# Hybrid decoder layer: the statistics of the query and key norm are copied out of PSUM with epsilon added, and the logarithm and the correction read the copy

## The chip, the core and the metric

The kernel runs on one core of a Trainium2 chip. A core has TensorE (PE, matrix products, results go to PSUM), VectorE (DVE), ScalarE (ACT), GpSimd (POOL) and SyncE (SP, which here issues most DMA transfers). Each engine works through a queue of its own in order; engines wait for each other by semaphores. The metric is the device time of one execution in microseconds (us), the median of several runs.

## What is computed

One inference step of one layer of a decoder for 520 tokens (512 of a prompt, 8 single decode tokens): an input projection, attention with 16 heads of 64 beside a short convolution, an output projection and an MLP. What matters here is the norm of the queries and keys, per head over its 64 elements:

```python
EPS = 1e-6
def _rmsnorm(x, g):
    xf = x.astype(jnp.float32)
    y = xf * lax.rsqrt(jnp.mean(xf * xf, axis=-1, keepdims=True) + EPS)
    return (y * g.astype(jnp.float32)).astype(x.dtype)

    q = _rmsnorm(q.reshape(b, s, N_HEADS, HEAD_DIM), q_g)
    k = _rmsnorm(k.reshape(b, s, N_HEADS, HEAD_DIM), k_g)
```

## The kernel before

Activations lie transposed, features on the 128 partitions and the 520 tokens in two halves of 260 columns (`HT`). A product of fp32 accuracy is made of three products of split operands (high x high, high x low, low x high). Weights come by DMA in tiles of 128 x 1024 (`raw`) and are split on the chip: ACT rounds the high part (L148), VectorE subtracts it to get the low part (L149). `block` (L210) issues six products for 128 rows of a tile, three split terms for each of the two halves; TensorE's products of the projections are at L213.

The order of work on every engine is the order in which the program issues it; it was written by hand. Small work of the attention is threaded between the products of the projections by generators: `block` calls `step` (L183) after every third product, and a `step` advances first the norm at the head of the queue `bgn` and then the generator at the head of `bg` by one `yield` each. `wait(n)` (L197) yields n times, so what stands behind `wait(3)` is issued nine products later than what stands before it. Being issued later does not by itself make work start later: it only stands behind more work in its engine's queue.

For each of eight pairs of heads j the projection makes q, k and v in turn. `ev_qkv` (L523) takes a result out of PSUM with VectorE (L530; for the first v at L528), squares it for q and k on ACT (L535) and GpSimd (L537, L538), and puts a `norm_gen` (L404) into `bgn` to start 24 steps later (30 for the first pair). `norm_gen` handles the two halves one after the other. Per half: two products with `bd`, a block-diagonal matrix of 1/64, put the mean squares of each head into a PSUM tile `st` (L408; it is taken from `pw`, which has two buffers); three steps later ACT takes the logarithm of mean plus epsilon (L411) and the exponential of -0.5 times that (L412), which gives a first reciprocal root r0; then VectorE makes one step of Newton's method and applies the gain (L414 to L417). After another three steps the second half or the end follows: ACT and VectorE split the normalised tile into high and low part (L419, L420). L414 is the last reader of `st`. The tiles r0 and t1 are in SBUF (name `h`, four buffers).

`attn_gen(j)` (L425) is queued when v of the pair is done. It waits in the program until both norms of j have been issued, then transposes the decode tokens' columns of q, k and v (L433, the second transpose reads the finished k) and v (L440), makes scores (L456), softmax (L463 to L473), transposes the probabilities into `pw` or `pS` tiles (L480), takes these out as high part on ACT (L483) and low part on VectorE (L484), and multiplies with v (L490); L495 and L496 take that result out. While the attention of pair j runs, the norms of pair j + 1 follow once the scores of j have been issued.

Of the kernel before, what the change touches and what calls it, by code (L numbers as in the profile page):

```python
# [25 lines left out]
F32 = mybir.dt.float32  # L26
F32R = mybir.dt.float32r
AF = mybir.ActivationFunctionType
OP = mybir.AluOpType
# [6 lines left out]
HT = TOK // 2  # L36
# [6 lines left out]
EPS = 1e-6  # L43
# [41 lines left out]
def hymba_kernel(ctx, tc, xT, wi, wo, wu, wd, state_k, state_v, sconv, relb, relrep, ohp, lcp, ohd, lcd,  # L85
                 gains, qkg, convw, yT, okT, ovT, ocp, oks, ovs, ocs):
    nc = tc.nc
    V, S, P, T, SP = nc.vector, nc.scalar, nc.gpsimd, nc.tensor, nc.sync
# [3 lines left out]
    wk = ctx.enter_context(tc.tile_pool(name="wk", bufs=1))  # L92
# [15 lines left out]
    def flat(t):  # L108
        return t.rearrange("p a b -> p (a b)")
# [87 lines left out]
    def wait(n):  # L197
        for _ in range(n):
            yield
# [4 lines left out]
    def wtile():  # L204
        return p2.tile([128, 512], F32, name="pw", bufs=2)
# [60 lines left out]
    epst = cst.tile([128, 1], F32, name="epst")  # L266
# [137 lines left out]
    def norm_gen(j, raw, sq, gain, hi, lo, k_out):  # L404
        for t in range(2):
            st = wtile()
            for i in range(2):
                T.matmul(st[:, :HT], bd, sq[i][:, t, :], start=i == 0, stop=i == 1)  # L408
            yield from wait(3)
            r0 = wk.tile([128, HT], F32, name="h", bufs=4)  # L410
            S.activation(r0, st[:, :HT], AF.Ln, bias=epst)  # L411
            S.activation(r0, r0, AF.Exp, scale=-0.5)  # L412
            t1 = wk.tile([128, HT], F32, name="h", bufs=4)
            V.scalar_tensor_tensor(t1, st[:, :HT], EPS, r0, op0=OP.add, op1=OP.mult)  # L414
            V.scalar_tensor_tensor(raw[:, t, :], raw[:, t, :], gain, r0, op0=OP.mult, op1=OP.mult)
            V.scalar_tensor_tensor(t1, t1, -0.5, r0, op0=OP.mult, op1=OP.mult)
            V.scalar_tensor_tensor(raw[:, t, :], t1, 1.5, raw[:, t, :], op0=OP.add, op1=OP.mult)  # L417
            yield from wait(3)
        S.activation(hi, flat(raw), AF.Copy)  # L419
        V.tensor_tensor(lo, flat(raw), hi.bitcast(F32), OP.subtract)  # L420
        if k_out is not None:
            SP.dma_start(k_out, flat(raw)[:, :SEQ])
        done["norm", j] = done.get(("norm", j), 0) + 1
# [99 lines left out]
    def ev_qkv(t, j, ps):  # L523
        raw = wt(name="raw")
        RAW[t, j] = raw
        if isinstance(ps, tuple):
            for h in range(2):
                V.tensor_tensor(raw[:, h], ps[h][:, :HT], rstd[:, h], OP.mult)  # L528
        else:
            V.tensor_tensor(raw, ps[:, :, :HT], rstd, OP.mult)  # L530
        if t == 1 and j:
            load_T(j)
        if t < 2:
            sh, sl_ = (wk.tile([128, 2, HT], F32R, name="sq", tag=g_, bufs=n_) for g_, n_ in (("w", 16), ("g", 4)))
            S.activation(sh, raw, AF.Square)  # L535
            sq = wt(name="tmp")
            P.tensor_tensor(sq, raw, raw, OP.mult)  # L537
            P.tensor_tensor(sl_, sq, sh.bitcast(F32), OP.subtract)  # L538
            hi, lo = (qh, ql) if t == 0 else (kh, kl)
            bgn.append([24 if j else 30, j, norm_gen(j, raw, (sh, sl_), qkgt[:, t:t + 1], hi, lo, okT[:, j] if t else None)])  # L540
        else:
            SP.dma_start(ovT[:, j], flat(raw)[:, :SEQ])
            bg.append(attn_gen(j))
# [534 lines left out]
    for n in range(7 * NG):  # L1078
# [18 lines left out]
        if kind == "up":  # L1097
# [27 lines left out]
            if gi == 2 and pi == 4:  # L1125
                st = p3.tile([128, 2, 512], F32, name="mn", bufs=2)
# [130 lines left out]
```

## Time and profile before

| | us |
|---|---|
| median of 3 runs (2150.16 to 2151.25) | 2150.71 |
| the profiled execution | 2150.38 |
| its span, first to last instruction | 2148.4 |
| TensorE busy in the span | 2129.5 |
| VectorE busy | 1758.7 |
| ScalarE busy | 957.8 |
| GpSimd busy | 56.6 |

The granted clock of TensorE is 1.00 in the whole span. The times of the projection of q, k and v with the norms and the attention of the prompt are about 47 to 405 us of the span. Times in the rows are microseconds from the start of the span. In a timeline a row gives start and length, the engine, the line, the operation, what it writes and reads and how many instructions it stands for; square brackets at its end give how long the engine had stood idle before it and for whom. Starts are exact; the lengths of neighbouring instructions overlap where an engine begins one before the last has been written out.

### The profile page before, as it was taken

The page shows a single profiled execution, that of the slowest core. Times are in us where ns is not written, and L with a number is a line of the kernel's source. Part 1 is how long each engine was busy: PE and PEld are TensorE (multiplying, and loading weights), DVE is VectorE, ACT ScalarE, POOL GpSimd, SP SyncE. Part 2 cuts the span into 40 slices and gives each one's busy share as a digit, 9 for nine tenths or more (in the row PEclk, how much of TensorE's full clock was granted, in tenths as well). Part 3 has the DMA queues.
Part 4 walks back from the last instruction along what each step waited for, and adds up shares of the span by engine and source line. Part 5 has one row for each costly group of instructions (what it writes and reads, how often), then busy time and mean ns, then how long its engine had stood idle before and what let it go on. Part 6 is the DMA issues. An engine that isn't in the chain of part 4 may idle for free.

```text
span 2148.4 us, 42322 instructions
## 1 busy us (share of the span) xinstructions
PE 2129.5 (99%) x17594; PEld 2103.1 (98%) x17594; DVE 1758.7 (82%) x2423; ACT 957.8 (45%) x1379; POOL 56.6 (3%) x81
## 2 busy tenths in 40 slices
PE   8999999999999999999999999999999999999999
PEld 8999999999999999999999999999999999999999
DVE  7777777697787657798888888888999999999997
ACT  5544444312123245554444444445444444444443
POOL 1010100000000000000000000000000000000000
PEclk9999999999999999999999999999999999999999
DMA  5354444476554647588785676676876666666653
GB/s 209 128 177 164 167 137 148 137 228 200 164 187 170 225 166 259 187 275 273 282 273 197 236 266 210 237 271 219 319 280 235 241 229 237 239 233 234 244 200 108
DMA packets 138367, 461.40 MB, mean 215 GB/s; under 512 B 19552, under 2 KB 49888, under 8 KB 131776
## 3 DMA queue, kind: packets, MB, share of 16 engines
q1 hardware_dynamic: 136320, 454.81, 60.7%
q0 software_dynamic: 1296, 3.67, 0.9%
q8 instruction: 138, 2.26, 0.4%
q14 instruction: 53, 0.43, 0.1%
q10 hardware_dynamic: 560, 0.22, 0.0%
HBM read 415.88 MB, written 181.16 MB: 278 GB/s over the span
## 4 chain that ended last, share of the span: by engine, by line
PE 89%; DVE 6%; ACT 2%; DMA 2%; issue 1%; SPq 0%; DVEq 0%; ACTq 0%
PE mn L1023 30%; PE mm L1023 29%; PE mm L213 26%; DMA raw<-wi 2%; DVE wlo L149 1%; PE pS L456 1%; PE pS L490 1%; DVE R L788 1%; PE pw L480 1%; ACT whi L148 1%; DVE x1t L927 0%; DVE acc L920 0%; DVE wlo L788 0%; ACT sq L918 0%; DVE kv L664 0%
## 5 line engine op out<-in xcount | busy, mean ns | idle before, releaser
L213 PE MATMUL mm<-R,whi 128*128 128x260 f32 x4000 | 676.6, 286 | 5.7 <-ACT whi L148 5.4
L213 PEld LDWEIGHTS mm<-R,whi 128*128 128x128 f32 x4000 | 559.4, 189 | 19.1 <-issue 8.6
L1023 PE MATMUL mm<-R,whi 128*128 128x260 f32 x3008 | 547.7, 283 | 1.2 <-ACT cs L1106 1.2
L1023 PE MATMUL mn<-R,whi 128*128 128x260 f32 x3008 | 547.7, 283 | 0.2 <-DVE yacc L1143 0.2
L1023 PEld LDWEIGHTS mm<-R,whi 128*128 128x128 f32 x3008 | 463.3, 188 | 1.5 <-ACT cs L1106 1.4
L1023 PEld LDWEIGHTS mn<-R,whi 128*128 128x128 f32 x3008 | 463.3, 188 | 0.4 <-issue 0.4
L1023 PE MATMUL mn<-R,wlo 128*128 128x260 f32 x1504 | 424.8, 282 | 0.7 <-DVE wlo L788 0.7
L1023 PE MATMUL mm<-R,wlo 128*128 128x260 f32 x1504 | 425.0, 283 | 0.4 <-DVE wlo L788 0.4
L213 PE MATMUL mm<-R,wlo 128*128 128x260 f32 x2000 | 403.1, 283 | 0.0
L788 DVE TENSOR_TENSOR wlo<-raw,whi 128x1024 fp32r<-128x1024 f32 x255 | 311.8, 1223 | 110.0 <-ACT whi L787 107.9
L787 ACT ACTIVATE whi<-raw 128x1024 fp32r<-128x1024 f32 x255 | 269.3, 1056 | 206.0 <-PE mn L1023 94.5
L213 PEld LDWEIGHTS mm<-R,wlo 128*128 128x128 f32 x2000 | 309.2, 189 | 0.4
L787 ACT ACTIVATE whi<-rg 128x1024 fp32r<-128x1024 f32 x186 | 197.3, 1061 | 217.0 <-PE mn L1023 87.5
L1023 PEld LDWEIGHTS mn<-R,wlo 128*128 128x128 f32 x1504 | 283.1, 188 | 0.9 <-DVE wlo L788 0.9
L1023 PEld LDWEIGHTS mm<-R,wlo 128*128 128x128 f32 x1504 | 283.1, 188 | 0.7 <-DVE wlo L788 0.6
L788 DVE TENSOR_TENSOR wlo<-rg,whi 128x1024 fp32r<-128x1024 f32 x186 | 226.5, 1218 | 2.1 <-ACT whi L787 2.0
L148 ACT ACTIVATE whi<-raw 128x1024 fp32r<-128x1024 f32 (+1 forms) x129 | 133.7, 1038 | 165.4 <-PE mm L213 129.7
L149 DVE TENSOR_TENSOR wlo<-raw,whi 128x1024 fp32r<-128x1024 f32 (+1 forms) x129 | 155.4, 1205 | 41.6 <-ACT whi L148 39.3
L841 DVE TENSOR_TENSOR raw<-raw 128x1024 f32<-128x1024 f32 x64 | 78.0, 1218 | 0.0
L841 DVE TENSOR_TENSOR raw<-rg,raw 128x1024 f32<-128x1024 f32 x62 | 76.0, 1225 | 2.1
L841 DVE TENSOR_TENSOR rg<-rg,raw 128x1024 f32<-128x1024 f32 x62 | 75.5, 1218 | 0.0
L1143 DVE TENSOR_TENSOR yacc<-mm,yacc 128x520 f32<-128x520 f32 x96 | 66.6, 694 | 7.0 <-PE mm L1023 6.0
(231 smaller groups left out, 2267.4 us busy)
## 6 DMA issues: line engine op xcount, KB each, us to landing
oks<-state_k SPq DMA_DIRECT2D x184, 356.0 KB
ovs<-state_v SPq DMA_DIRECT2D x184, 356.0 KB
raw<-wi SPq DMA_DIRECT2D x94, 512.0 KB
raw<-wu SPq DMA_DIRECT2D x64, 512.0 KB
rg<-wd SPq DMA_DIRECT2D x64, 512.0 KB
raw<-wd SPq DMA_DIRECT2D x64, 512.0 KB
rg<-wu SPq DMA_DIRECT2D x60, 512.0 KB
raw<-wo SPq DMA_DIRECT2D x32, 512.0 KB
```

The lines of the kernel that those rows point to most:

```text
L148: S.activation(his[i][:, h], raws[i][:, h], AF.Copy)
L149: V.tensor_tensor(los[i][:, h], raws[i][:, h], his[i][:, h].bitcast(F32), OP.subtract)
L213: T.matmul(ps[t][:, :HT] if isinstance(ps, tuple) else ps[:, t, :HT], a[:, k, :], b[:, t, :], start=start and n == 0, stop=stop and n == 2)
L456: T.matmul(ss[hp][:, :w], a[r, q], b[r, :w], start=n == 0, stop=n == 2)
L480: T.transpose(st[:, s * 128:(s + 1) * 128], lg[:, s * 128:(s + 1) * 128], ident)
L490: T.matmul(st[:, s * 128:], vv[:, hp, s].rearrange("p c e -> p (c e)"), b[:, s, s * 128:], start=s == 0 and n == 0, stop=s == 3 and n == 1 ...
L787: S.activation(hi, src, AF.Copy)
L788: eng.tensor_tensor(lo, src, hi.bitcast(F32), OP.subtract)
L841: V.tensor_tensor(o_, a_, b_, op)
L1023: T.matmul(ps[:, r, :HT], a[:, k, :], b(kt), start=n % 7 in ((0, 1, 3) if kts == 8 else (0, 1)) and kt == 0 and m == 0, stop=kt == kts - 1 ...
L1143: V.tensor_tensor(dst[:, r], v[:, r], dst[:, r], OP.add)
```

## The change

The two statements of `norm_gen` that read `st` become one. An addition on VectorE, issued right behind the products and ahead of the three steps of waiting, writes mean plus epsilon to the SBUF tile t1. The logarithm reads t1 instead of `st` and has no bias operand any more. Where L414 had added epsilon and multiplied by r0 in one instruction on `st`, a multiplication of t1 by r0 remains. t1 is taken from `h` before r0 instead of after it. The other VectorE steps, and everything else, stay.

```diff
             st = wtile()
             for i in range(2):
                 T.matmul(st[:, :HT], bd, sq[i][:, t, :], start=i == 0, stop=i == 1)
+
+            t1 = wk.tile([128, HT], F32, name="h", bufs=4)
+            V.tensor_scalar(t1, st[:, :HT], EPS, None, op0=OP.add)
             yield from wait(3)
             r0 = wk.tile([128, HT], F32, name="h", bufs=4)
-            S.activation(r0, st[:, :HT], AF.Ln, bias=epst)
+            S.activation(r0, t1, AF.Ln)
             S.activation(r0, r0, AF.Exp, scale=-0.5)
-            t1 = wk.tile([128, HT], F32, name="h", bufs=4)
-            V.scalar_tensor_tensor(t1, st[:, :HT], EPS, r0, op0=OP.add, op1=OP.mult)
+            V.tensor_tensor(t1, t1, r0, OP.mult)
             V.scalar_tensor_tensor(raw[:, t, :], raw[:, t, :], gain, r0, op0=OP.mult, op1=OP.mult)
             V.scalar_tensor_tensor(t1, t1, -0.5, r0, op0=OP.mult, op1=OP.mult)
             V.scalar_tensor_tensor(raw[:, t, :], t1, 1.5, raw[:, t, :], op0=OP.add, op1=OP.mult)
```

## Rows read from the trace of the kernel before

**Rows 1.** The page: busy time of TensorE and its weight loads, share of the span.

```profile
PE 2129.5 (99%) x17594; PEld 2103.1 (98%) x17594; DVE 1758.7 (82%) x2423; ACT 957.8 (45%) x1379; POOL 56.6 (3%) x81
```

**Rows 2.** Busy time by stretch: stretch, length, each engine's time; the sum covers 47 to 410.

```profile
210.00:370.00 160.00, 159.73 (x1301) 153.22 (x1300) 114.92 (x274) 78.12 (x164) 16.67 (x15) 1.00 0.46 151
...
sum 363.00, PE 358.64 PEld 341.82 DVE 261.80 ACT 172.98 POOL 33.98; mean PE 59.77 PEld 56.97 DVE 43.63 ACT 28.83 POOL 5.66
```

**Rows 3.** TensorE's waits in the whole span: us in total, times, longest.

```profile
PE pw L408 <- DVE h L414: 1.5, 3, 0.9
...
PE pw L433 <- DVE raw L417: 1.0, 2, 0.6
```

**Rows 4.** Groups by line, 47 to 370 us: busy us, mean ns of one, idle before.

```profile
L411 ACT ACTIVATE h<-pw,epst 128x260 f32<-128x260 f32 x32 | 15.0, 470 | 12.5 <-PE pw L408 12.1
...
L414 DVE SCALAR_TENSOR_TENSOR h<-pw,h 128x260 f32<-128x260 f32 x32 | 13.6, 425 | 10.3 <-ACT h L412 9.9
L412 ACT ACTIVATE h<-h 128x260 f32<-128x260 f32 x32 | 13.5, 422 | 1.0
```

**Rows 5.** Timeline of VectorE, ScalarE and TensorE: head pair 0, norm of k.

```profile
58.93 0.42 DVE L414 SCALAR_TENSOR_TENSOR h<-pw,h 128x260 f32<-128x260 f32 x1
...
60.13 0.43 DVE L417 SCALAR_TENSOR_TENSOR raw<-h,raw 128x260 f32<-128x260 f32 x1
60.47 0.42 DVE L414 SCALAR_TENSOR_TENSOR h<-pw,h 128x260 f32<-128x260 f32 x1
...
58.39 0.46 ACT L411 ACTIVATE h<-pw,epst 128x260 f32<-128x260 f32 x1
...
62.15 0.38 PE L433 MATMUL pw<-ident,raw 128*8 128x128 f32 x2 [0.60 <-DVE raw L417]
```

**Rows 6.** Timeline: head pair 6, norm of k.

```profile
322.33 0.48 ACT L411 ACTIVATE h<-pw,epst 128x260 f32<-128x260 f32 x1 [1.44 <-PE pw L408]
...
322.12 0.43 DVE L417 SCALAR_TENSOR_TENSOR raw<-h,raw 128x260 f32<-128x260 f32 x1
...
323.30 0.42 DVE L414 SCALAR_TENSOR_TENSOR h<-pw,h 128x260 f32<-128x260 f32 x1
...
324.63 0.72 PE L433 MATMUL pw<-ident,raw 128*8 128x128 f32 x3
```

**Rows 7.** Timeline: head pair 6, norm of q and the transposes behind it.

```profile
303.96 1.23 DVE L149 TENSOR_TENSOR wlo<-raw,whi 128x1024 fp32r<-128x1024 f32 x1 [0.39 <-ACT whi L148]
...
307.79 0.70 DVE L530 TENSOR_TENSOR raw<-mm,rstd 128x520 f32<-128x520 f32 x1 [0.46 <-PE mm L213]
310.08 0.43 DVE L414 SCALAR_TENSOR_TENSOR h<-pw,h 128x260 f32<-128x260 f32 x1 [1.59 <-ACT h L412]
...
313.67 0.42 DVE L484 TENSOR_TENSOR R<-pw,R 128x256 fp32r<-128x256 f32 x1
...
314.15 0.66 PE L480 MATMUL pw<-ident,lg 128*128 128x128 f32 x4
```

**Rows 8.** Timeline: head pair 2, norms of q and k.

```profile
126.45 1.34 DVE L473 TENSOR_SCALAR lg<-lg,sm 128x512 f32<-128x512 f32 x1
...
131.59 0.50 PE L490 MATMUL pS<-R 128*128 128x512 f32 x1 [0.43 <-DVE R L484]
...
141.14 0.65 PE L480 MATMUL pw<-ident,lg 128*128 128x128 f32 x4 [0.80 <-DVE R L484]
```

**Rows 9.** Timeline: head pair 1, norms of q and k and the transposes L433.

```profile
84.71 0.49 DVE L473 TENSOR_SCALAR lg<-lg,sm 128x512 f32<-128x512 f32 x1
...
85.81 0.51 PE L408 MATMUL pw<-sq,bd 128*128 128x260 f32 x2 [0.19 <-DVE h L414]
...
100.43 0.50 PE L490 MATMUL pS<-R 128*128 128x512 f32 x1 [0.24 <-DVE R L484]
...
103.73 0.49 PE L433 MATMUL pw<-ident,raw 128*8 128x128 f32 x3
```

**Rows 10.** Timeline: head pair 3, end of the norm of k.

```profile
190.85 0.38 PE L433 MATMUL pw<-ident,raw 128*8 128x128 f32 x2 [0.41 <-DVE raw L417]
```

## The prediction

> **What bounds the kernel now.** I read the page first: TensorE is busy 99% of the span [rows 1]. Then the table of stretches, for the stage in which the changed lines run, 47 to 370 us, taken on to 410 us: TensorE is busy 358.64 of 363.00 us, so 4.36 us are all that an edit there can win from its idle time, and in 210 to 370 us it is 0.27 us [rows 2]. The stage is therefore bound by TensorE's products, and what matters of VectorE (DVE) and ScalarE (ACT) is only where TensorE comes to a point at which it needs their result. The waits of TensorE name these points [rows 3]: the next statistics product waits for a buffer of pw until L414 has read it (1.5 us in 3 waits), the transposes at L433 wait for the finished k, L417 (1.0 us), and by the timeline the transposes at L480 wait for a pw buffer until L484 has emptied it (0.80 us), the products at L490 for the low part that L484 writes [rows 8, 9]. The last three are chains in which VectorE works in the order of its queue. A point that waits already has no slack: what makes VectorE later there is paid by TensorE in full.
>
> **The change, part by part.** There are 16 norms (q and k for eight head pairs j), each in two halves: 32 times the edit. Removed is one read of PSUM by ACT and the fused add-multiply L414. Added is an addition on VectorE, and the multiplication stays. Durations [rows 4]: L414 reads PSUM at this shape in 0.43 us, L411 reads PSUM in 0.47 us, L412 reads SBUF at the same shape in 0.42 us.
>
> The multiplication has L414's shape and takes its 0.43 us: no change. The logarithm now reads SBUF: I take L412's 0.42 us, between 0.42 and 0.47. [...] L411 and L412 differ in function too, but the rows have the SBUF read the shorter one, and I go by them.
>
> The addition has no row of its own kind. From below: a one-operand VectorE instruction on 512 columns of SBUF takes 0.49 us [rows 9], half of which, 0.25 us, is an estimate for 260 columns. From above: one on 512 columns took 1.34 us in a stretch with GpSimd at work [rows 8]. I take L414's 0.43 us, the row with the same source and shape.
>
> As mere load, 32 x 0.43 = 13.8 us on VectorE would be hidden: VectorE is busy 115 of 160 us in the quiet stretch [rows 2]. What counts is where the addition stands. It is issued right behind the product, three steps ahead of the old Ln, and VectorE's queue is in order, so it must first finish all that was issued earlier. Before, Ln and Exp ran on ACT while VectorE worked that off. Now Ln waits for the addition, and the multiplication, which stands behind it on VectorE, waits for Exp: VectorE, ACT, VectorE, one after another. One such round: from Ln's start to L414's start it is now 0.97 us when nothing is in the way (322.33 to 323.30) [rows 6]; less 0.05 for the SBUF read is 0.92, plus 0.43 for the addition and 0.03 for a hand-over is a round of 1.38 us. Where VectorE was late anyway, the addition gets L414's old place and the multiplication comes the whole 1.38 us later. Where both engines were free and TensorE's product started the chain, it comes 1.38 - 0.97 = 0.41 us later.
>
> *Head pair 0, k.* ACT had done both logarithms at 58.85 us, long before VectorE came to them. VectorE finishes L420 (issued before k's first product), then L414 at 58.93 [rows 5]. Now the first addition is at 58.93 and everything behind it 1.38 us later; the second addition stands behind the first half's L417, is again in L414's place, and costs another 1.38. L433, which waits 0.60 us already, waits 2.8 us longer: **+2.8 us**.
>
> *Head pairs 4 to 7* repeat one pattern to 0.1 us; 6 stands for them. k is a free chain: in the first half +0.41. The second addition stands behind the first half's L417, which then starts at 322.53; the next instruction follows 0.34 us later as L414 follows L417 in [rows 5], at 322.87, and the multiplication at 324.25 instead of 323.30 [rows 6]. The three transposes at L433 take 0.72 us there where three unhindered ones take 0.49 [rows 9], so there is no slack: +0.95. In q, the first addition stands behind L149 (ends 305.19), the first half ends 0.8 us later, and the second addition comes before L530, which moves from 307.79 to about 308.4; the square behind it and then Ln follow on ACT, so L414's place moves from 310.08 to 310.57. VectorE works without a break from there to L484 at 313.67 (its end, 314.09, is what L480 at 314.15 waits for): +0.49 [rows 7]. Sum 1.44, four times: **+5.8 us**.
>
> *Head pair 2, q.* VectorE is late: its L473 takes until 127.79 and the addition takes L414's place. So the wait of the second product for pw stays what it is, since the addition ends when L414 ended. Behind it come a round of idle VectorE (0.95 us until Exp is done), the four old steps, L484, L149, then the second addition (0.34) and only then the L484 whose result L490 waits for at 131.59: 1.38 + 0.34 = 1.7 us. In k the same: the addition behind L149, L484 a round later, and L480 at 141.14, which waits 0.80 us for it already, 1.4 us later [rows 8]. **+3.1 us**.
>
> *Head pair 1.* The first addition stands behind L473 (ends 85.20), so by the same steps the q halves end 1.2 and 1.6 us later, k's 1.9 and 3.0 us later, and all of it reaches L484 before L490 at 100.43, which waits already (0.24 us) [rows 9]: **+3.0 us**. L433 has over 6 us of slack here and costs nothing.
>
> *Head pair 3.* q as in pair 2 and 6: 1.6 us. k: the first half a round later (behind L149), the second catches up behind L530: 0.55 us at L433, which waits 0.41 already [rows 10]. **+2.2 us**.
>
> Sum: 2.8 + 5.8 + 3.1 + 3.0 + 2.2 = 16.9 us. Off goes the one wait for pw that the earlier release ends, 0.19 us at head pair 1 [rows 9] (those at 2 and 3 stay): 16.7 us. The profiled execution took 2150.38 us (its span 2148.4 and 2 us around it), 0.33 us under the median; with 16.7 us it is 2167.1, on the median 2167.4. After 410 us TensorE waits for nothing whose time is fixed (in the table of waits all its waits are for ACT and VectorE), so nothing gives the delay back. I say 2167.
>
> **Rivals.** *The release of pw wins.* The addition frees PSUM without waiting for ACT. [...] Here L408's waits for L414 are 1.5 us in all; with L433's and L480's gone too it would be 3.3 us, 2147.1 us, and even all 4.36 idle us give 2146.0. For it: three waits are of that kind. Against it: in two of them L414 began as soon as VectorE was free, so an addition in its place ends no sooner, and in 210 to 370 us there is no such wait. It decides only if VectorE stands idle when the product ends. 2147, chance 0.06, of which 0.03 for a gain of over 0.2%.
>
> *All is hidden.* If TensorE reaches L433, L480 and L490 late enough, VectorE's rounds cost nothing: 2151 us. For it: VectorE is idle 28% of the quiet stretch. Against it: in head pairs 0, 2 and 3 these points wait already. Also here: that the addition does not stand where the code puts it. Chance 0.09.
>
> *Only the exposed ends cost.* The rounds are made up inside q and in pairs 1 to 3, and just L433 pays: 2.8 at pair 0 and 4 x 0.95: 6.6 us, 2157 us. Chance 0.13.
>
> **How the numbers follow.** Forecast 0.72. About 0.2%, 4.3 us, is what a measurement of this kernel can tell from no change. The range goes down to the exposed ends alone, 2157 us. Upwards, if each of the 16 norms paid a full round, 16 x 1.38 = 22.1 us, 2173 us. The shorter addition of 0.25 us makes a round 1.20 and the sum 14.5 us, 2165, within it. Faster by over 0.2%: 0.03. Within 0.2%: 0.12 (all hidden, and a release that wins little). Slower: 0.85.
>
> **What would show it.** VectorE 13 to 14 us busier, ACT about 1.5 us less. Ln's idle time ended by the addition, the multiplication's by Exp, in most halves. TensorE's waits at L433 for the last norm step about 2.8 us in pair 0 and 1 us in 4 to 7, waits at L480 and L490 for L484 up to 1.7 us, TensorE's idle in 47 to 410 us near 20 us against 4.36, nothing changed after 410 us but the start. Wrong would be: additions that start while VectorE would have stood idle and end before ACT is free, L433 without a longer wait, or TensorE stalls for weights: the splits L148 and L149 behind the norms come up to 3 us later, which I count as nothing since a split is issued half a weight tile and one whole tile, 72 products, ahead of its use; with that cover gone each such stall is added.

## The result, and the profile after

The changed kernel takes 2172.29 us (median, 2171.11 to 2172.45) against 2150.98 us (2150.16 to 2151.51) for the kernel before in the same rounds: ratio 1.0099, 95% interval 1.0087 to 1.0111. It is 21.3 us slower. The forecast was 2167, with a range of 2157 to 2173. The profiled execution took 2172.15 us, its span is 2170.4 us, 22.0 us above that of before.

The page of the changed kernel, busy times (the line that answers to [rows 1]):

```profile
PE 2133.4 (98%) x17594; PEld 2104.3 (97%) x17594; DVE 1773.6 (82%) x2455; ACT 956.9 (44%) x1379; POOL 56.4 (3%) x81
```

VectorE has its 32 more instructions, 14.9 us more. The table of stretches of the changed kernel (stretch, length, TensorE, weight loads, VectorE, ScalarE, GpSimd, granted clock, DMA) shows where the time lies:

```profile
47.00:430.00 383.00, 361.59 (x2901) 342.29 (x2900) 275.67 (x662) 171.47 (x366) 33.89 (x33) 1.00 0.42 141
430.00:2171.00 1741.00, 1732.26 (x14414) 1725.42 (x14412) 1462.83 (x1734) 755.05 (x967) 12.91 (x36) 1.00 0.66 229
```

TensorE now stands idle for 21.4 us between 47 and 430 us, where it was 4.36 us up to 410 [rows 2]; behind that nothing has changed but the start. Its waits, changed kernel (us in all, times, longest; the helper lines are two higher than before, so L435 is the old L433, L482 the old L480, L486 the old L484, L492 the old L490, L419 the last norm step):

```profile
PE pw L435 <- DVE raw L419: 9.0, 6, 3.3
...
PE pw L482 <- DVE R L486: 5.2, 6, 2.2
PE pS L492 <- DVE R L486: 4.8, 4, 1.9
...
PE pw L408 <- DVE h L411: 1.3, 2, 0.8
...
PE pw L482 <- DVE h L411: 1.1, 1, 1.1
```

The waits for a free `pw` at L408 are hardly shorter (1.3 us against 1.5 [rows 3]), and L482 now waits 1.1 us in pair 1 for a buffer that an addition has not emptied yet. The three kinds of wait that the prediction priced have grown to 19 us. ScalarE's logarithm waited for the addition in 26 of the 32 halves (40.3 us), the multiplication for the exponential in 30 (20.5 us); where VectorE stood idle ahead of an addition, 12.7 us in 5 times, it was for the product at L408, never for a tile of `h`. Head pair 0 shows the round trip undisturbed. Timelines of VectorE, ScalarE and TensorE, changed kernel (L411 addition, L414 logarithm, L415 exponential, L416 multiplication):

```profile
59.76 0.42 DVE L411 TENSOR_SCALAR h<-pw 128x260 f32<-128x260 f32 x1
61.12 0.43 DVE L416 TENSOR_TENSOR h<-h 128x260 f32<-128x260 f32 x1 [0.94 <-ACT h L415]
...
62.67 0.42 DVE L411 TENSOR_SCALAR h<-pw 128x260 f32<-128x260 f32 x1
64.03 0.43 DVE L416 TENSOR_TENSOR h<-h 128x260 f32<-128x260 f32 x1 [0.94 <-ACT h L415]
...
60.22 0.42 ACT L414 ACTIVATE h<-h 128x260 f32<-128x260 f32 x1 [1.71 <-DVE h L411]
...
63.13 0.42 ACT L414 ACTIVATE h<-h 128x260 f32<-128x260 f32 x1 [2.04 <-DVE h L411]
...
65.72 0.59 PE L435 MATMUL pw<-ident,raw 128*8 128x128 f32 x2 [3.32 <-DVE raw L419]
```

From the first addition to the first multiplication it is 1.36 us, of which VectorE stands idle 0.94 us, waiting for an exponential on an engine that had itself waited 1.71 us for the addition. Before the change the first logarithm had ended 0.9 us and the second 1.6 us before VectorE came to L414 of its half. In the changed kernel the second half repeats the round, because its addition stands behind the first half's last step. TensorE waits 3.32 us where it waited 0.60.

### The profile page after: what moved, and what is told of

The parts are those of the page before. It is cut to its first block, busy times and chain, and to the rows that moved or that the text cites. A ratio compares the mean times of both kernels' runs of the same rounds, so it can differ in the third digit from the quotient of the medians.

```text
span 2170.4 us, 42384 instructions
## 1 busy us (share of the span) xinstructions
PE 2133.4 (98%) x17594; PEld 2104.3 (97%) x17594; DVE 1773.6 (82%) x2455; ACT 956.9 (44%) x1379; POOL 56.4 (3%) x81
## 4 chain that ended last, share of the span: by engine, by line
PE 84%; DVE 9%; ACT 3%; DMA 2%; issue 1%; SPq 0%; DVEq 0%; ACTq 0%
PE mn L1025 29%; PE mm L1025 29%; PE mm L213 23%; DVE wlo L149 2%; DMA raw<-wi 1%; PE pS L458 1%; ACT whi L148 1%; DVE h L416 1%; DVE R L790 1%; ACT h L415 1%; DVE raw L419 1%; DVE raw L417 1%; PE pS L492 1%; ACT h L414 1%; DVE h L411 0%
## 5 line engine op out<-in xcount | busy, mean ns | idle before, releaser
L148 ACT ACTIVATE whi<-raw 128x1024 fp32r<-128x1024 f32 (+1 forms) x129 | 133.7, 1039 | 163.6 <-PE mm L213 134.1
L149 DVE TENSOR_TENSOR wlo<-raw,whi 128x1024 fp32r<-128x1024 f32 (+1 forms) x129 | 155.5, 1206 | 39.7 <-ACT whi L148 38.9
```

The source lines that it names most:

```text
L148: S.activation(his[i][:, h], raws[i][:, h], AF.Copy)
L149: V.tensor_tensor(los[i][:, h], raws[i][:, h], his[i][:, h].bitcast(F32), OP.subtract)
```

## The experiments

Delays below are worked out by setting the n-th product of TensorE in one trace against the n-th in the other; both have 17594. A delay is how much later the product comes than in the kernel before. Where a version issues products in another order (L433 later, below) the figure is rough.

**Out of PSUM by ScalarE instead of VectorE.** The kernel before with

```diff
+            t1 = wk.tile([128, HT], F32, name="h", bufs=4)
+            S.activation(t1, st[:, :HT], AF.Copy)
             r0 = wk.tile([128, HT], F32, name="h", bufs=4)
-            S.activation(r0, st[:, :HT], AF.Ln, bias=epst)
+            S.activation(r0, t1, AF.Ln, bias=epst)
             S.activation(r0, r0, AF.Exp, scale=-0.5)
-            t1 = wk.tile([128, HT], F32, name="h", bufs=4)
-            V.scalar_tensor_tensor(t1, st[:, :HT], EPS, r0, op0=OP.add, op1=OP.mult)
+            V.scalar_tensor_tensor(t1, t1, EPS, r0, op0=OP.add, op1=OP.mult)
```

> The statistics leave PSUM by a plain copy on ScalarE, issued right ahead of the logarithm; logarithm and L414 (addition and multiplication fused, as before) read the copy. PSUM is read once, as in the change, by one more instruction per half, as in the change, but nothing goes VectorE to ScalarE and back. Theory of the round trip (the addition waits in VectorE's queue and the logarithm for it): most of the 21 us are gone; what stays is 0.45 us per free half and the multiplication held up by GpSimd, in pairs 4 to 7 about 0.45 at L433 and 0.4 at L480: 2156 us, 2153 to 2160. Rival, the extra instruction and the detour through SBUF cost by themselves: 2165 to 2172.

Measured: 2155.79 us, ratio 1.0023 (1.0014 to 1.0033), +4.9 us. One instruction more per half, the same detour through SBUF, PSUM released ahead of the correction too, and three quarters of the loss are gone. What distinguishes it is the engine: copy and logarithm follow each other on ScalarE and nothing goes from VectorE to ScalarE and back. The copy also stands three steps later than the addition, but with the addition in that place the kernel is slower still (below), so the place does not explain the gain. Pair 0 pays 0.15 us here (0.75 us at L434 for 0.60). The waits of TensorE in this kernel (L434 is the old L433, L481 the old L480, L491 the old L490):

```profile
PE pw L434 <- DVE raw L418: 3.4, 6, 0.7
PE pw L481 <- DVE R L485: 2.9, 6, 1.2
PE pS L491 <- DVE R L485: 2.8, 4, 1.5
```

The waits at L408 for `pw` have vanished altogether from the table, so the early release does work when it doesn't wait for VectorE; but in pair 2 TensorE wins 1.1 us there and loses 1.1 us at L491 three us later, because VectorE, which is late, has not written the low part any sooner.

**One more VectorE instruction, no hand-over.** The kernel before with a spare multiplication by 1 at the addition's place; it reads the half of q or k in SBUF, not `st`, so it does not wait for TensorE's product either:

```diff
                 T.matmul(st[:, :HT], bd, sq[i][:, t, :], start=i == 0, stop=i == 1)
+            V.tensor_scalar(raw[:, t, :], raw[:, t, :], 1.0, None, op0=OP.mult)
             yield from wait(3)
```

> The kernel before with one more VectorE instruction per half at the place of the addition (a multiplication of the half of q or k by 1, in SBUF), on which nobody on ScalarE waits; logarithm and L414 read PSUM as before. Theory of the round trip: only places where VectorE is late anyway pay its 0.35 to 0.4 us, some 0.7 at pair 0, 1 to 1.2 in pairs 1 to 3 and 0.15 each in 4 to 7: +4.6 us, 2155.5, 2152 to 2158. Rival, VectorE's load and place in the queue are the cost: 2165 to 2172.

Measured: 2152.80 us, ratio 1.0009 (0.9999 to 1.0018), +1.9 us, at the edge of what can be told from no change. The group's row:

```profile
L409 DVE TENSOR_SCALAR raw<-raw 128x260 f32<-128x260 f32 x31 | 8.9, 289 | 0.0
```

The instruction took 0.29 us, not the 0.35 to 0.4 reckoned with (and not the addition's 0.42, so it is a lower bound). 9 us of load on VectorE cost TensorE some 2 us: load alone is mostly hidden, as the prediction had it. Whether it costs something that the addition makes VectorE wait for the product, this version doesn't show; the one with the addition three steps later does.

**Pair 0 alone.** The change only where `j == 0`.

> The change in head pair 0 alone, the other seven as before. Theory: two rounds of 1.38 us at L433 (2.7 us), then a TensorE that stood idle over 3 us runs at a granted clock of 0.5 for about 2.5 us, which costs another 1.2 us: +3.9 us, 2154.9, and the row of the granted clock in the 2 us behind L433 shows 0.5. Rival, the dip of the clock has another cause than this wait: +2.7 us, 2153.7, or a dip without it.

Measured: 2155.67 us, ratio 1.0022 (1.0012 to 1.0031), +4.8 us, more than the theory's 3.9. In the profiled execution the delay grows by 2.5 us at L433 and by another 2.6 us in the 6 us behind it, in which every product takes about twice as long. Stretches of this kernel (granted clock is the third figure from the right):

```profile
66.00:68.00 2.00, 2.00 (x12) 2.00 (x11) 1.46 (x2) 1.21 (x2) 0.00 (x0) 0.50 0.78 221
68.00:70.00 2.00, 2.00 (x11) 2.00 (x11) 1.07 (x2) 0.89 (x2) 0.85 (x1) 0.50 0.96 322
70.00:72.00 2.00, 2.00 (x14) 1.74 (x13) 1.12 (x2) 1.54 (x3) 1.53 (x2) 0.60 0.31 119
72.00:74.00 2.00, 2.00 (x20) 1.95 (x17) 1.73 (x9) 0.77 (x4) 0.00 (x0) 1.00 0.91 301
```

11 or 12 products in 2 us against 20: after it stood idle 3.13 us, TensorE runs at a granted clock of 0.50 instead of 1.00. Of the ten executions the one with a mean granted clock of 1.000 took 2153.91 us, near the 2153.7 of the rival without the clock; the two at 0.998 took 2156.6 us. The same fall in the changed kernel, where it lasts less long and costs 1.3 us:

```profile
66.00:68.00 2.00, 2.00 (x11) 2.00 (x10) 1.39 (x2) 1.28 (x2) 0.00 (x0) 0.50 0.80 193
68.00:70.00 2.00, 2.00 (x17) 2.00 (x16) 1.15 (x2) 0.82 (x2) 0.77 (x1) 0.85 0.91 330
```

**L433 later.** The changed kernel with `yield from wait(5 if j else 20)` for `wait(1 if j else 10)` ahead of L433.

> The changed kernel with the transposes at L433 issued later: ten more steps in pair 0 (20 for 10), four more in the others (5 for 1). Theory: TensorE's waits there are gone (2.7 + 1.2 by the clock in pair 0, 0.8 in pair 3, 1.05 in each of 4 to 7), those at L480 and L490 in the norm of q stay: 2172.3 - 9 = 2163, 2161 to 2165. Rival, the delay only moves on to the next place that needs the finished k (L456): 2170 to 2173.

Measured: 2173.86 us, ratio 1.0102 (1.0085 to 1.0119): nothing won, just above the rival's 2170 to 2173. In pair 0 the theory's part came true: no wait there, the granted clock 1.00 from 55 to 76 us, about 4.7 us ahead of the changed kernel by 78 us. From then on it is given back and more, as the attention of each pair now runs four or ten steps later beside the next norms; not at L456, where the rival put it. The waits at the old L433 have gone from the table, and these have taken their place:

```profile
PE pS L492 <- DVE R L486: 7.6, 7, 1.9
...
PE pw L408 <- DVE h L411: 5.3, 4, 1.7
PE pw L482 <- DVE R L486: 3.8, 3, 2.2
PE pw L482 <- DVE h L411: 3.4, 3, 1.2
PE pS L492 <- ACT R L485: 2.1, 1, 2.1
```

L408 and L482 wait for a `pw` buffer that an addition has not emptied yet, although nothing but VectorE's queue holds it up. So the delay of VectorE is met wherever TensorE needs something of it next; the place was not the cause. The mean granted clock of this profiled execution is 0.998, so with 1.00 from 55 to 76 us it fell elsewhere. That does not hide a gain: the execution of this kernel with a mean granted clock of 1.000 has a span of 2169.6 us, that of the changed kernel 2169.1.

**k alone.** The change only in the norms of k.

> The change in the norms of k alone, those of q as before. From the delays read off the changed kernel's trace: 2.7 at L433 of pair 0 and 1.2 or more by the clock behind it, about 1 in pair 1, 1.4 at L480 of pair 2, 0.7 in pair 3 and 1.05 at L433 in each of 4 to 7: +11.2 us, 2162, 2160 to 2164. Rival, q and k share one backlog of VectorE and neither half alone pays: under 2156.

Measured: 2163.52 us (2161.98 to 2165.39), ratio 1.0058 (1.0043 to 1.0073), +12.5 us; in the profiled execution 11.6 us, of which 0.95 lie before 30 us and are not the change's (see the start-up below): 2.7 in pair 0, 1.5 in pair 1, 1.4 in pair 2, 0.8 in pair 3 and 1.0 to 1.1 in each of 4 to 7. In pair 0, at L480 of pair 2 and at L433 of pairs 3 to 7 that is the figure that the changed kernel has at the same place (without the clock). If the parts add, q's share is the remaining 9 us; a version with the change in q alone was not run. This profiled execution waited 3.29 us in pair 0 and kept its clock:

```profile
62.00:66.00 4.00, 0.71 (x8) 0.41 (x7) 2.72 (x8) 1.08 (x3) 0.00 (x0) 1.00 0.00 0
66.00:68.00 2.00, 2.00 (x20) 2.00 (x19) 1.32 (x2) 1.35 (x2) 0.00 (x0) 1.00 0.72 190
```

Its four executions have spans of 2160.0, 2161.5, 2162.0 and 2163.5 us at mean granted clocks of 1.000, 0.999, 0.999 and 0.998. So whether the clock falls after such a wait differs from execution to execution, and the spread goes with it. Of the changed kernel's four, the three at 0.999 have 2170.4 to 2170.7 us and the one at 1.000 has 2169.1.

**The addition three steps later.** The changed kernel with the addition behind `yield from wait(3)`, right ahead of the logarithm.

> The changed kernel with the addition issued three steps later, right ahead of the logarithm, so that it stands in the place where L414 stood less what ScalarE took. Theory: the cost is the hand-over from VectorE to ScalarE and back behind VectorE's queue, and the three steps change little: 2172, 2169 to 2175. Rival, the early place is the cost (VectorE held up by an addition that waits for TensorE): under 2162.

Measured: 2185.54 us, ratio 1.0156 (1.0139 to 1.0173), +34.5 us. Neither theory: the early place is not the cost, it is what keeps the cost down. The 12.7 us that VectorE stood idle ahead of early additions, for TensorE's product, are gone here, and the kernel is slower. VectorE in pair 6, norm of k (L412 is the addition here, L532 the old L530), and TensorE behind it:

```profile
353.02 0.69 DVE L532 TENSOR_TENSOR raw<-mm,rstd 128x520 f32<-128x520 f32 x1
353.63 0.42 DVE L412 TENSOR_SCALAR h<-pw 128x260 f32<-128x260 f32 x1
354.98 0.43 DVE L416 TENSOR_TENSOR h<-h 128x260 f32<-128x260 f32 x1 [0.94 <-ACT h L415]
...
356.67 0.38 PE L435 MATMUL pw<-ident,raw 128*8 128x128 f32 x2 [2.29 <-DVE raw L419]
```

The addition now stands behind the 0.7 us of L532, which in the changed kernel runs inside the round, while ScalarE has it. So L435 waits 2.29 us instead of 1.12, and behind six of the eight waits at L435 and L482 of 1.8 us and more the granted clock falls to 0.50 (behind 3.54, 1.82, 2.20, 2.29, 2.30 and 2.29 us, not behind 2.19 and 2.31). Read off the delays, the clock takes 9 to 10 us in this profiled execution, 1.3 in that of the changed kernel: some 8 of the 15 us between the two. This was the slowest of four; the other three have mean granted clocks of 0.996 and 0.997 against its 0.994, so the clock takes less in them. Some 7 us are left for the later place itself.

**Without GpSimd.** Both kernels with GpSimd's two operations per norm (L537, L538) replaced by fills with zero, which read nothing; the statistics then lack the low part of the squares.

> The kernel before with GpSimd's two operations per norm (square of q or k and its low part) replaced by two fills with zero, which read nothing: the statistics then lack the low part of the squares. Theory: GpSimd held up VectorE (L415 0.88 for 0.48 us, L473 1.3 for 0.5 us); without it the waits of pair 2 at L408 and L490 go: 2149, 2148 to 2150.5.

> The changed kernel with the same replacement; the statistics lack the low part of the squares. Theory: the multiplication has two operands in SBUF and is held until GpSimd is done (1.28 for 0.43 us in the second half of q in pairs 3 to 7); without that the waits of 0.7 us at L480 in these pairs and the 1.7 us at L490 of pair 2 go: 2166.5, 2164 to 2168.5, so 17 to 18 us above the kernel before in the same form instead of 21. Rival, GpSimd has no part in it: 21 us above it.

Measured: 2149.08 us (ratio 0.9990, 0.9981 to 0.9999) and 2167.66 us (1.0078, 1.0063 to 1.0093): 18.6 us apart instead of 21.3. Part of the two expectations failed: in pair 2 the wait at L408 went, but that at L490 stayed at 0.39 us in the kernel before and at 1.57 us in the changed one, so GpSimd makes little of it. In the changed kernel, pair 6, second half of q, VectorE and GpSimd:

```profile
328.28 1.27 DVE L416 TENSOR_TENSOR h<-h 128x260 f32<-128x260 f32 x1 [1.53 <-ACT h L415]
...
327.96 1.30 POOL L540 TENSOR_TENSOR sq<-tmp,sq 128x520 fp32r<-128x520 f32 x1
```

The multiplication ends 0.29 us after GpSimd's operation, not before. In the kernel before it was L415 that was held so, and L414 at 310.08 [rows 7], one of whose operands is in PSUM, kept its 0.43 us:

```profile
310.42 0.87 DVE L415 SCALAR_TENSOR_TENSOR raw<-raw,qkgt,h 128x260 f32<-128x260 f32 x1
```

Groups of the multiplication, changed kernel and changed kernel without GpSimd (busy us, mean ns):

```profile
L416 DVE TENSOR_TENSOR h<-h 128x260 f32<-128x260 f32 x32 | 17.9, 561 | 20.5 <-ACT h L415 20.5
```

```profile
L416 DVE TENSOR_TENSOR h<-h 128x260 f32<-128x260 f32 x32 | 13.7, 429 | 20.2 <-ACT h L415 20.2
```

The waits of 0.6 us at L482 in pairs 3 to 7 are gone in the second; those at L435 stay at 1.1. The two totals don't differ by this alone: without GpSimd the clock kept its level in pair 0 and fell in pair 2, the changed kernel the other way round. Beside GpSimd's second operation L415 took 0.87 us for 0.48 and L416 1.27 for 0.43, both with their 128 x 260 operands in SBUF, and L414, with one of them in PSUM, its usual 0.43.

**A version that beats both?** The kernel before with the transposes of L433 in the order q, v, k, and the same with 12 steps for 10 in pair 0.

> The kernel before with the three transposes at L433 in the order q, v, k instead of q, k, v: TensorE comes to the one that waits for the finished k one transpose, 0.1 us, later. Theory (TensorE's waits at L433 are paid in full): 0.1 to 0.12 us less in each of pairs 0 and 3 to 7, 0.6 us in all: 2150.3, at the edge of what can be measured. Rival, v is finished later than k somewhere: no change or slower.

> The same, with L433 of pair 0 issued two steps later (12 for 10). Theory: the 0.6 us that TensorE waits there in the kernel before go too, if the two steps later bring no new wait in the norms of pair 1: 2149.8, 2149 to 2150.5. Rival, later steps of pair 0 run into the norms of pair 1, as with ten steps in the changed kernel: 2151 to 2152.

Measured: 2150.56 us (ratio 0.9999, 0.9990 to 1.0008) and 2152.68 us (1.0007, 0.9998 to 1.0016). The first is no change that can be measured; in the second, waits at L408 grow from 1.5 to 3.1 us, the rival's way, and the time is above the rival's 2151 to 2152. None of these beats the kernel before while computing the same.

## Why the prediction was right, and where it was off

Delay of TensorE in the profiled execution of the changed kernel, by the terms of the sum:

| term | predicted us | measured us |
|---|---|---|
| pair 0 | 2.8 | 2.7, and 1.3 by the clock |
| pair 1 (less 0.19) | 2.8 | 3.1 |
| pair 2 | 3.1 | 3.1 |
| pair 3 | 2.2 | 2.8 |
| pairs 4 to 7 | 5.8 | 7.9 |
| start-up, before 30 us | 0 | 0.9 |
| sum (measured: with 0.2 in small pieces) | 16.7 | 21.9 |

**The mechanism** stood: a round from VectorE to ScalarE and back of 1.38 us by the sum, 1.36 measured (the hand-over, 0.03 in the sum, is 0.04 us from the addition's end at 60.18 to the logarithm's start at 60.22); in pair 0 twice, in pair 2 behind L473 and again behind L149, each at the place that was named. No stall for weights came: TensorE's waits for the split at L148 are 5.5 us against 5.4. The copy on ScalarE shows that the hand-over makes the loss, the spare instruction that load is little of it.

**What counts is where the addition stands**: right in kind, but the prediction named it only as a cost. The later place is worse by 13 us in the medians, and about half of that is the clock, going by the profiled executions; the early one lets L530 run while ScalarE works.

**The release of pw wins**: it failed for the reason given. The addition ended when L414 had ended, so two of three waits stayed (1.3 us of 1.5). Where ScalarE empties PSUM they vanish, and the gain is lost at the next thing that VectorE is late for.

**"The multiplication has L414's shape and takes its 0.43 us: no change"** was the step that failed. It has the shape but not the memory: both operands are in SBUF, and GpSimd's work holds it, 1.27 us for 0.43 in the second half of q in pairs 3 to 7 (mean of all 0.561 us, without that work 0.429); that is 0.4 us more than L415 had lost there before. In each of pairs 4 to 7 the delay is 0.7 us at L480, where 0.49 was forecast, 1.0 to 1.1 at L433 for 0.95, and 0.2 at L490, for which the sum has no term and whose cause stays open: 7.9 for 5.8. Without GpSimd's work the delay at L480 is gone altogether, so how its 0.7 us divide between the hold and the later L530 is not shown.

**The clock** was not in the sum at all. A wait of 3 us was priced at 3 us; in some executions it costs up to 2.6 more.

**The range** held in part by luck. Its upper end, 2173, came from a full round for each of the 16 norms; what took the time to within 1 us of it was something else, mainly the hold by GpSimd and the clock, which the sum did not have.

**The logarithm** took 0.42 us (0.419 in the changed kernel) as reckoned, but not for the reason given. With its bias operand it takes 0.47 from PSUM [rows 4] and, in the kernel with the copy on ScalarE, 0.51 from SBUF; the copy itself takes 0.38 from PSUM, against 0.42 for an exponential from SBUF:

```profile
L413 ACT ACTIVATE h<-h,epst 128x260 f32<-128x260 f32 x32 | 16.5, 514 | 1.0
...
L411 ACT ACTIVATE h<-pw 128x260 f32<-128x260 f32 x32 | 12.2, 380 | 10.2 <-PE pw L408 9.8
```

The two logarithms with bias, 0.514 and 0.470 us, differ only in where they read: the one from SBUF is the longer by 0.044 us, where the prediction took the read from SBUF for the shorter; what the change won back is the bias operand, 0.095 us (0.514 to 0.419, both from SBUF).

**The start-up** is not the change's: at the product that comes at 39.94 us in the profiled execution of before, all eleven other kernels are between 40.36 and 41.10, those among them that are no slower than before. That execution was an early one.

## What to carry to other kernels

Before a PSUM tile is emptied early, ask whose queue the emptying stands in and who then waits for it: a short step on a late engine ahead of a chain on an idle one turns two parallel queues into a round trip, here 1.4 us for an instruction of 0.4; 4.9 us in all where ScalarE did the emptying, 21.3 where VectorE did. When an operand moves from PSUM to SBUF, look for GpSimd at work beside the instruction and at the operands' memory, not at the shape alone: here 1.27 us for 0.43. And put a price on each long wait of TensorE for the clock behind it, here up to 2.6 us behind a wait of 3.13.

## What was not expected of the hardware

At some of its waits TensorE's granted clock fell to 0.50 and stayed there for 3 to 6 us behind the wait. It was so after waits of 3.32, 3.13 and 3.54 us in pair 0 of three kernels, after 2.19 us in pair 2 of the changed kernel without GpSimd, and in the kernel with the later addition also after 1.82, 2.20 and three times 2.3 us. It was not so after 3.29 and 3.22 us in pair 0 of the kernel with k alone and the changed kernel without GpSimd, after 2.18 us in pair 2 of the changed kernel, nor after 2.19 and 2.31 us in pairs 2 and 7 of the one with the later addition. The length of the wait alone doesn't decide it; what does stays open.

A plain bias operand, 128 x 1, makes ScalarE's logarithm of 260 columns 0.095 us longer (0.514 to 0.419 us, both from SBUF).
